# Gate/up of a SwiGLU block as a 2x2 block product with seven products, and the FFN in three parts

## Chip, cores and metric

The kernel runs on one core of a Trainium2 chip. The metric is the device time of one execution in microseconds (us), from the first to the last work of the program; the kernel before has a median of 799.0 us over 3 runs (798.96, 799.0 and 799.23).

## The reference

One transformer-like layer over 512 latent tokens of width 1024 with 256 context tokens. A mixer (attention and a gated recurrence) comes first and isn't touched by the change. The rest is an FFN with 2816 inner features, that is 22 feature tiles of 128, and a last norm:

```python
x = x + gt1 * mix_lat
h2 = modulate(rmsnorm(x, g_norm_ffn[layer]), sh2, sc2)
x = x + gt2 * swiglu(h2, w_gate[layer], w_up[layer], w_down[layer])
return rmsnorm(x, g_final)

def swiglu(h, w_gate, w_up, w_down):
    return (jax.nn.silu(h @ w_gate) * (h @ w_up)) @ w_down
```

All of it is in float32.

## The kernel before, in words

Features lie on the 128 partitions and tokens on the free axis. So that the products keep float32 accuracy, each operand is split into a high part of type fp32r and a low part, which is the rest, and `mm3` (L148) issues three matmuls per 128x128 weight tile: high by high (L150), high by low (L151), low by high (L152).

Weights come in units of 128x1024. `make_unit` (L119) fetches a unit by a DMA on SP's queue into `wf` (three buffers), ACT casts it to the high part `wh` (L132), DVE subtracts it for the low part `wl` (L133). `unit` and `prefetch` make units two or three ahead of their use. A unit holds the eight k-tiles of one feature tile of gate or up, or eight (the last six) of the 22 k-tiles of one output tile of down.

The normalised input h2 is written as `h2h` and `h2l` by `norm2` (L949), first for tokens 0 to 255, then for 256 to 511. `gu_mm` (L989) makes the 24 matmuls of gate or up for one tile, into the two halves of a PSUM tile `big` (two buffers). `gu_act` (L994) then takes silu on ACT, multiplies with up on DVE (L997), and splits into `ah` and `al` (L998 on ACT, L999 on DVE), which hold all 22 tiles. Tiles 0 and 1 run in two halves of 256 tokens, the second beside `norm2(256)`; tiles 2 to 21 have 512 columns. Behind each of these `mods(1)` issues a piece of a modulation vector that is needed later (`late_mod`, L422: a DMA and a DVE product of 128x1024, L427), eight in all.

`ffn_down` (L1020) makes an output tile of 66 matmuls of 512 columns in a PSUM tile `sm` (four buffers), adds it to `x1` (L1028, DVE) and squares it for the last norm (L934 on ACT, L936 on DVE). There are eight; the last runs in two halves of 256 tokens. `final` (L1035) is the last norm of one half: sums over partitions on PE (L174), the inverse root on ACT and DVE (L190 to L182), spread by PE (L216), eight products on DVE (L1041), and the output's DMAs (L1045). `final(0)` is put into the list `side`, which `tick` takes steps from, and so runs beside the last 66 matmuls; `final(256)` comes after them.

The order on each engine is set by the framework's scheduler from the order in which the code issues things and from its own priorities: each engine then runs its list in order and waits at each instruction for what it needs.

Of the kernel before, what the change touches and what calls it, by code (L numbers as in the profile page):

```python
# [10 lines left out]
F32 = mybir.dt.float32  # L11
F32R = mybir.dt.float32r
# [6 lines left out]
P = 128  # L19
# [33 lines left out]
def block_kernel(ctx: ExitStack, tc: tile.TileContext, xT, ctxT, vec, cin, cst, msk, wm, wmt, wi, wqkv, wo, wgu, wd, out):  # L53
# [56 lines left out]
    for u in range(2 * FT):  # L110
        units.append(("wgu", wgu[u], UNIT))
    for n in range(KT):
        for part in range(3):
            w = UNIT if part < 2 else DFF - 2 * UNIT
            units.append(("wd", wd[n][:, part * UNIT : part * UNIT + w], w))
    made = []
    stage = {"pool": L0, "f": 3, "s": 3}

    def make_unit(i):  # L119
        kind, src, w = units[i]  # L120
        f = L0.tile([P, UNIT], F32, tag="wf", name=nm("wf"), bufs=3)
        nc.sync.dma_start(f[:, :w], src)
        if kind == "wo" and i >= WO0 + 4:
            hi = stage["pool"].tile([P, UNIT], F32R, tag="rh", name=nm("rh"), bufs=4)
            lo = stage["pool"].tile([P, UNIT], F32R, tag="rl", name=nm("rl"), bufs=4)
        elif i == GU0 + 3:
            hi = N2.tile([P, UNIT], F32R, tag="xh", name=nm("xh"), bufs=1)
            lo = N2.tile([P, UNIT], F32R, tag="xl", name=nm("xl"), bufs=1)
# [3 lines left out]
        nc.scalar.copy(hi[:, :w], f[:, :w])  # L132
        nc.vector.tensor_sub(lo[:, :w], f[:, :w], hi[:, :w].bitcast(F32))  # L133
        made.append((hi, lo))

    WO0 = NW_IN + 4
    GU0 = WO0 + 8
    WD0 = GU0 + 2 * FT

    def prefetch(n):  # L140
        while len(made) < min(n, len(units)):
            make_unit(len(made))

    def unit(i, ahead=2):
        prefetch(i + 1 + ahead)
        return made[i]

    def mm3(o, L, R, start, stop):  # L148
        (lh, ll), (rh, rl) = L, R
        nc.tensor.matmul(o, lh, rh, start=start, stop=False, skip_group_check=True)  # L150
        nc.tensor.matmul(o, lh, rl, start=False, stop=False, skip_group_check=True)  # L151
        nc.tensor.matmul(o, ll, rh, start=False, stop=stop, skip_group_check=True)  # L152

    def sl(t, f):
        return f(t[0]), f(t[1])
# [771 lines left out]
    def add_sq(key, src, n):  # L927
        if n == 0:
            t = N2.tile([P, 256], F32, tag=f"sqa{key}", name=nm("sqa"), bufs=1)
            sqa[key] = [t]  # L930
            nc.scalar.activation(t, src, AF.Square)
        else:
            t = N2.tile([P, 256], F32, tag="sqt", name=nm("sqt"), bufs=4)
            nc.scalar.activation(t, src, AF.Square)  # L934
            if n < KT - 1:
                nc.vector.tensor_add(sqa[key][0], sqa[key][0], t)  # L936
            else:
                sqa[key].append(t)
# [26 lines left out]

# [17 lines left out]
    side.append(norm2(256))  # L983

    FF = pool("FF", "left")
    ah = FF.tile([P, FT, NL], F32R, name="ah")
    al = FF.tile([P, FT, NL], F32R, name="al")

    def gu_mm(ps, j, u, a, w):  # L989
        for k in range(KT):  # L990
            L = sl(u, lambda t: t[:, k * P : (k + 1) * P])
            mm3(ps[:, j, a : a + w], L, (h2h[:, k, a : a + w], h2l[:, k, a : a + w]), k == 0, k == KT - 1)

    def gu_act(n, ps):  # L994
        sg = FF.tile([P, NL], F32, tag="sgl", name=nm("sgl"), bufs=2)
        nc.scalar.activation(sg, ps[:, 0, :], AF.Silu)
        nc.vector.tensor_mul(sg, sg, ps[:, 1, :])  # L997
        nc.scalar.copy(ah[:, n, :], sg)  # L998
        nc.vector.tensor_sub(al[:, n, :], sg, ah[:, n, :].bitcast(F32))  # L999

    us = [unit(GU0 + i, 3 - i) for i in range(4)]
    pp = [big(), big()]
# [3 lines left out]
            tick()  # L1006
    drain()
    sqa.clear()
    for n in range(2):
        for j in range(2):  # L1010
            gu_mm(pp[n], j, us[2 * n + j], 256, 256)
        gu_act(n, pp[n])
    for n in range(2, FT):
        ps = big()
        for j in range(2):
            gu_mm(ps, j, unit(GU0 + 2 * n + j), 0, NL)
        gu_act(n, ps)
        mods(1)

    def ffn_down(n, a, w):  # L1020
        us = [unit(WD0 + 3 * n + j, 2 - j) for j in range(3)]
        ps = sm()
        for k in range(FT):
            L = sl(us[k // 8], lambda t: t[:, (k % 8) * P : (k % 8 + 1) * P])
            mm3(ps[:, :w], L, (ah[:, k, a : a + w], al[:, k, a : a + w]), k == 0, k == FT - 1)
            if k in (3, 9):
                tick()
        nc.vector.scalar_tensor_tensor(x1[:, n, a : a + w], ps[:, :w], mod[:, 3, n : n + 1], x1[:, n, a : a + w],  # L1028
                                       op0=ALU.mult, op1=ALU.add)
# [129 lines left out]
```

## Time and profile before

| what | value |
|---|---|
| median of the runs | 799.0 us (798.96 to 799.23) |
| the profiled execution, first to last instruction (span) | 793.8 us |
| mean granted TensorE clock | 0.992 |
| PE busy | 771.1 us (97%) |
| DVE busy | 447.4 us (56%) |
| ACT busy | 311.3 us (39%) |
| POOL busy | 7.8 us (1%) |
| gate/up and down | from about 400 us to 783 us |

Durations of single instructions are in nanoseconds where a row says "mean", all else in microseconds. A matmul's row shows 0.40 or 0.28 us, but matmuls overlap in PE's pipeline: what one costs is the distance between the starts of two. The profiled execution has no other time than its span; the runs' median lies 5.2 us above it.

### The profile page before, as it was taken

The numbers are of one execution on the slowest core, as the hardware profiler recorded it, in microseconds if no ns is written. First come the engines' busy times: TensorE is split into PE (matmuls) and PEld (weight loads), VectorE is DVE, ScalarE is ACT, GpSimd is POOL, SyncE is SP. The second block draws the span as 40 slices with busy tenths as digits, with TensorE's granted clock in tenths as the row PEclk, the third lists the DMA queues.
The fourth block names the chain that finished last, engine by engine and source line by source line (L and its number), as shares of the span: only waits on it lengthen the run. The fifth ranks groups of instructions, "written<-read, shape, count | busy, mean of one in ns | idle before, by whom it ended". The sixth has DMA issues, their size and how long they took to land.

```text
span 793.8 us, 10825 instructions
## 1 busy us (share of the span) xinstructions
PE 771.1 (97%) x4342; PEld 629.0 (79%) x4342; DVE 447.4 (56%) x820; ACT 311.3 (39%) x569; POOL 7.8 (1%) x15
## 2 busy tenths in 40 slices
PE   8899999999999989999999999999999999999995
PEld 6568888788887667777999888888888888888885
DVE  5576569739788998885656344423333333233324
ACT  6244345434553587654444233222322232222211
POOL 0000000000000000000000000000000000000000
PEclk8999999999999999999999999999999999999998
DMA  8924723321110023335402334333222323332303
GB/s 329 390 83 140 237 81 107 133 81 54 40 54 28 28 80 107 107 132 194 178 2 80 132 133 159 132 109 97 89 105 82 105 74 100 92 91 84 102 16 107
DMA packets 26706, 88.77 MB, mean 112 GB/s; under 512 B 2976, under 2 KB 5280, under 8 KB 26528
## 3 DMA queue, kind: packets, MB, share of 16 engines
q1 hardware_dynamic: 25568, 87.03, 31.6%
q10 hardware_dynamic: 1088, 1.05, 0.4%
q8 instruction: 34, 0.56, 0.3%
q14 instruction: 16, 0.13, 0.0%
HBM read 85.97 MB, written 2.10 MB: 111 GB/s over the span
## 4 chain that ended last, share of the span: by engine, by line
PE 87%; DVE 6%; DMA 4%; ACT 2%; issue 1%; SPq 0%; DVEq 0%; ACTq 0%
PE big L150 17%; PE big L151 16%; PE big L152 16%; PE sm L150 9%; PE sm L151 9%; PE sm L152 9%; PE big L853 3%; DMA xc<-in_ctxT_dram 1%; PE sm L872 1%; PE sm L604 1%; PE big L854 1%; DMA wm<-in_wm_dram 1%; DMA wms<-in_wm_dram 1%; DVE U L585 1%; PE sm L598 1%
## 5 line engine op out<-in xcount | busy, mean ns | idle before, releaser
L133 DVE TENSOR_TENSOR wl<-wf,wh 128x1024 fp32r<-128x1024 f32 (+2 forms) x100 | 119.7, 1197 | 186.0 <-ACT wh L132 185.9
L132 ACT CAST wh<-wf 128x1024 fp32r<-128x1024 f32 (+2 forms) x100 | 102.9, 1029 | 280.7 <-PE big L151 167.9
L150 PE MATMUL big<-h2h,wh 128*128 128x512 f32 (+1 forms) x368 | 140.3, 381 | 0.0
L151 PE MATMUL big<-h2l,wh 128*128 128x512 f32 (+1 forms) x368 | 140.0, 381 | 0.0
L152 PE MATMUL big<-h2h,wl 128*128 128x512 f32 (+1 forms) x368 | 140.0, 381 | 0.0
L152 PEld LDWEIGHTS big<-h2h,wl 128*128 128x128 f32 x368 | 69.2, 188 | 14.6
L150 PEld LDWEIGHTS big<-h2h,wh 128*128 128x128 f32 x368 | 69.2, 188 | 14.5
L151 PEld LDWEIGHTS big<-h2l,wh 128*128 128x128 f32 x368 | 69.2, 188 | 14.4
L150 PE MATMUL sm<-ah,wh 128*128 128x512 f32 (+1 forms) x198 | 73.5, 371 | 0.0
L152 PE MATMUL sm<-ah,wl 128*128 128x512 f32 (+1 forms) x198 | 73.4, 371 | 0.0
L151 PE MATMUL sm<-al,wh 128*128 128x512 f32 (+1 forms) x198 | 73.4, 370 | 0.0
L427 DVE SCALAR_TENSOR_TENSOR wl<-wl,cs 128x1024 f32<-128x1024 f32 x32 | 39.1, 1222 | 33.2 <-DMA wl<-in_wmt_dram 33.1
L150 PE MATMUL big<-wh,hh 128*128 128x512 f32 x96 | 40.1, 421 | 3.3 <-ACT hh L340 1.9
L150 PEld LDWEIGHTS sm<-ah,wh 128*128 128x128 f32 x198 | 37.3, 188 | 7.1
L151 PEld LDWEIGHTS sm<-al,wh 128*128 128x128 f32 x198 | 37.3, 188 | 7.1
L152 PEld LDWEIGHTS sm<-ah,wl 128*128 128x128 f32 x198 | 37.3, 188 | 7.1
L150 PE MATMUL big<-hh,wh 128*128 128x512 f32 x104 | 42.8, 412 | 0.0
L151 PE MATMUL big<-hl,wh 128*128 128x512 f32 x104 | 40.9, 393 | 0.0
L152 PE MATMUL big<-hh,wl 128*128 128x512 f32 x104 | 40.8, 392 | 0.0
L151 PE MATMUL big<-wl,hh 128*128 128x512 f32 x96 | 38.6, 404 | 0.0
L152 PE MATMUL big<-wh,hl 128*128 128x512 f32 x96 | 38.4, 402 | 0.0
L506 DVE RECIPROCAL G<-S 128x528 f32<-128x528 f32 x8 | 27.5, 3435 | 0.1
(323 smaller groups left out, 1349.5 us busy)
## 6 DMA issues: line engine op xcount, KB each, us to landing
wf<-in_wgu_dram SPq DMA_DIRECT2D x44, 512.0 KB, 3.3
wl<-in_wmt_dram SPq DMA_DIRECT2D x32, 512.0 KB, 3.3
wf<-in_wi_dram SPq DMA_DIRECT2D x25, 512.0 KB, 4.3
wf<-in_wd_dram SPq DMA_DIRECT2D x16, 512.0 KB, 3.5
wms<-in_wm_dram SPq DMA_DIRECT2D x11, 512.0 KB, 9.9
wf<-in_wo_dram SPq DMA_DIRECT2D x8, 512.0 KB, 3.3
wf<-in_wd_dram SPq DMA_DIRECT2D x8, 384.0 KB, 3.0
wm<-in_wm_dram SPq DMA_DIRECT2D x5, 512.0 KB, 10.3
```

Source lines behind the costliest of these rows:

```text
L132: nc.scalar.copy(hi[:, :w], f[:, :w])
L133: nc.vector.tensor_sub(lo[:, :w], f[:, :w], hi[:, :w].bitcast(F32))
L150: nc.tensor.matmul(o, lh, rh, start=start, stop=False, skip_group_check=True)
L151: nc.tensor.matmul(o, lh, rl, start=False, stop=False, skip_group_check=True)
L152: nc.tensor.matmul(o, ll, rh, start=False, stop=stop, skip_group_check=True)
L427: nc.vector.scalar_tensor_tensor(f, f, 1.0, sc, op0=ALU.mult, op1=ALU.mult, accum_out=acc)
L506: nc.vector.reciprocal(I, S)
L585: nc.vector.scalar_tensor_tensor(U[:, c1, :], U[:, c0, :], er[:, 1, c0 : c0 + 1], U[:, c1, :], op0=ALU.mult, op1=ALU.add)
L598: nc.tensor.matmul(t, a2[:, j, :], vt[:, j, h * P : (h + 1) * P], start=True, stop=False, skip_group_check=True)
L604: nc.tensor.matmul(t[g * CH : (g + 1) * CH, :], qg[:, c, :], U[:, c, :], start=False, stop=(g == 1 and d == 1), skip_group_check=True, til ...
L853: nc.tensor.matmul(ps[:, 0, :], L, R[:, :NL], start=(i == 0), stop=(i == 4), skip_group_check=True)
L854: nc.tensor.matmul(ps[:, 1, :NC], L, R[:, NL:], start=(i == 0), stop=(i == 4), skip_group_check=True)
```

## The change

Tiles 0 to 2 stay as they were (`PLAIN = 3`). For tiles 3 to 21 gate and up are seen as one 2x2 block product: the two rows are gate and up, the inner dimension is cut into k-tiles 0 to 3 and 4 to 7, the columns are the tokens 0 to 255 and 256 to 511. Winograd's form of Strassen's product gets the four blocks from seven products of half the size, each of 4 k-tiles by 256 tokens (`gu_pair`: 84 matmuls of 256 columns, where there were 48 of 512). What it needs beside them:

- Sums of weight blocks, once per tile (`make_pair`): s0 and s3 on POOL, s1 and s2 on DVE, in one buffer `ss`; then the casts on ACT and low parts on DVE of four tiles: y (s0, s1), x (the gate unit, tags `wh`, `wl`), z (s2, s3), q (the second half of the up unit).
- Sums of token blocks, once (`h2_sums`): four blocks from h2 on DVE, split into `th` and `tl`. `norm2` writes a float32 copy of h2's second token half for this (`h2f`).
- Sums of products: some are taken in PSUM (a product adds to what is there); the others by copies of a product on ACT (`keep`) and additions on DVE of 256 columns (L1111, L1114, L1117; L1119 and L1122 multiply silu(gate) with up). A product into a half of `big` waits until the product before it in that tile has been read.

The FFN is cut into three parts of 8, 8 and 6 feature tiles: gate/up of a part, then its down product, which adds to `x1`. `ah` and `al` hold one part. The squares are taken in the last part. The steps of `make_pair` are issued by `feed` between the products. The late modulation pieces go two behind each of the tiles 3 to 6. `sqt` has two buffers, before four.

```diff
+    def make_pair(src):
+        fg, fu = [L0.tile([P, UNIT], F32, tag="wf", name=nm("wf"), bufs=3) for _ in range(2)]
+        nc.sync.dma_start(fg, src[0])
+        nc.sync.dma_start(fu, src[1])
+        yield
+        ss = FF.tile([P, 4, 512], F32, tag="ss", name=nm("ss"), bufs=1)
+        nc.gpsimd.tensor_add(ss[:, 0, :], fu[:, :512], fu[:, 512:])
+        nc.gpsimd.tensor_sub(ss[:, 3, :], fg[:, :512], fu[:, :512])
+        yield
+        nc.vector.tensor_sub(ss[:, 1, :], ss[:, 0, :], fg[:, :512])
+        nc.vector.tensor_sub(ss[:, 2, :], fg[:, 512:], ss[:, 1, :])
+        yield
...
+            nc.scalar.copy(hi, src)
+            nc.vector.tensor_sub(lo, src, hi.bitcast(F32))
...
+        y = split(FF, "y", s2[:, :UNIT], 1)
+        yield
+        x = split(L0, "w", fg, 3)
+        yield
+        z = split(FF, "z", s2[:, UNIT:], 1)
+        yield
+        q = split(FF, "q", fu[:, 512:], 1)
...
             nc.scalar.activation(h2h[:, n, a : a + w], t, AF.Identity, bias=s)
+            if a:
+                nc.scalar.activation(h2f[:, n, :], t, AF.Identity, bias=s)
...
+    def h2_sums():
+        yield
+        tr = FF.tile([P, 4, 4, 256], F32, tag="ah", name="tr", bufs=1)
...
+        nc.vector.tensor_sub(tr[:, 2], b22, b12)
+        nc.vector.tensor_sub(tr[:, 0], b12, q(h2h, 0))
+        nc.vector.tensor_sub(tr[:, 0], tr[:, 0], q(h2l, 0))
+        yield
+        nc.vector.tensor_sub(tr[:, 1], b22, tr[:, 0])
+        nc.vector.tensor_sub(tr[:, 3], q(h2h, 1), tr[:, 1])
+        nc.vector.tensor_add(tr[:, 3], tr[:, 3], q(h2l, 1))
+        for i in (0, 1, 2, 3):
...
+            nc.scalar.copy(th[:, i], f)
+            nc.vector.tensor_sub(tl[:, i], f, th[:, i].bitcast(F32))
...
+        prod(pa, a11, lambda k: hq(0, k), True, True)
+        k1 = keep(pa)
+        feed()
+        prod(pb, s1, tq(0), True, True)
+        k5 = keep(pb)
+        feed()
+        prod(pa, s2, tq(1), False, True)
+        k6 = keep(pa)
+        feed()
+        prod(pb, s4, h22, False, True)
+        nc.vector.tensor_add(sg[:, 256:], pb, k6)
+        feed()
+        prod(pa, s3, tq(2), False, True)
+        nc.vector.tensor_add(up, pa, k5)
+        feed()
+        prod(pc, a12, lambda k: hq(1, k), True, True)
+        nc.vector.tensor_add(sg[:, :256], pc, k1)
+        nc.scalar.activation(sg, sg, AF.Silu)
+        nc.vector.tensor_mul(sg[:, 256:], sg[:, 256:], up)
+        feed()
+        prod(pa, a22, tq(3), False, True)
+        nc.vector.tensor_mul(sg[:, :256], sg[:, :256], pa)
+        gu_split(n, sg)
+        feed()
...
+    for n in range(2, KT):
+        gu(n)
+    for n in range(KT):
+        ffn_down(0, n, 0, NL)
+    for n in range(KT, 2 * KT):
+        gu(n)
+    for n in range(KT):
+        ffn_down(1, n, 0, NL)
+    for n in range(2 * KT, FT):
+        gu(n)
...
     for n in range(KT - 1):
-        ffn_down(n, 0, NL)
-    ffn_down(KT - 1, 0, 256)
+        ffn_down(2, n, 0, NL)
+    ffn_down(2, KT - 1, 0, 256)
     side.append(final(0))
-    ffn_down(KT - 1, 256, 256)
+    ffn_down(2, KT - 1, 256, 256)
     side.append(final(256))
```

What stands in a row on DVE in the middle of gate/up, before: the low parts of two units (L133), the product with up (L997), the low part of the activation (L999), tile after tile. Operands are the output, then behind the arrow the inputs.

```order
L133 TENSOR_TENSOR wl_706_5036<-wf_704_5033,wh_705_5035 128x1024
L133 TENSOR_TENSOR wl_711_5072<-wf_709_5069,wh_710_5071 128x1024
L997 TENSOR_TENSOR sgl_707_5063<-sgl_707_5063,big_700_5002 128x512
L999 TENSOR_TENSOR al_3970<-sgl_707_5063,ah_3969 128x512
L133 TENSOR_TENSOR wl_714_5102<-wf_712_5099,wh_713_5101 128x1024
```

And now, in part 2, one turn from the low part of one pair's y to that of the next (lines of the changed kernel: L146 low parts, L137 and L138 the sums s1 and s2, L1073 the activation's low part, the other L11xx evictions of products). The PSUM tile big_789 belongs to the pair ahead, big_807 to the pair whose weights are yl_798, zl_802 and ql_804, and ss_812 to the pair behind.

```order
L146 TENSOR_TENSOR yl_798_5584<-ss_794_5550,yh_797_5583 128x1024
L146 TENSOR_TENSOR wl_818_5728<-wf_805_5655,wh_817_5727 128x1024
L1111 TENSOR_TENSOR sgl_791_5534<-big_789_5532,keep_796_5581 128x256
L1114 TENSOR_TENSOR up_792_5535<-big_789_5532,keep_795_5565 128x256
L1119 TENSOR_TENSOR sgl_791_5534<-sgl_791_5534,up_792_5535 128x256
L146 TENSOR_TENSOR zl_802_5618<-ss_794_5550,zh_801_5617 128x1024
L1122 TENSOR_TENSOR sgl_791_5534<-sgl_791_5534,big_789_5532 128x256
L146 TENSOR_TENSOR ql_804_5637<-wf_788_5529,qh_803_5636 128x512
L137 TENSOR_TENSOR ss_812_5677<-ss_812_5677,wf_805_5655 128x512
L1073 TENSOR_TENSOR al_768_5398<-sgl_791_5534,ah_767_5397 128x512
L138 TENSOR_TENSOR ss_812_5677<-wf_805_5655,ss_812_5677 128x512
L146 TENSOR_TENSOR yl_816_5711<-ss_812_5677,yh_815_5710 128x1024
```

Four rows have become eleven or twelve, and evictions of one pair, which PE waits for, now stand in line with the weight work of the next two. L137 stands behind POOL's addition into the same buffer `ss`, and that behind `zl_802`, the last reader of the buffer's former content.

On PE at a boundary between two tiles, before: the last matmuls into one `big`, then the first into the other.

```order
L150 MATMUL big_732_5266<-h2h_3496,wh_729_5233 128x512
L151 MATMUL big_732_5266<-h2l_3497,wh_729_5233 128x512
L152 MATMUL big_732_5266<-h2h_3496,wl_730_5234 128x512
L150 MATMUL big_740_5332<-h2h_3496,wh_734_5269 128x512
L151 MATMUL big_740_5332<-h2l_3497,wh_734_5269 128x512
L152 MATMUL big_740_5332<-h2h_3496,wl_735_5270 128x512
```

And now between two products of one pair: the last matmul of product s4 (zh, zl with h2), then what stands between, then the first of product s3 (zh with th), which waits for L1111 of this pair on DVE.

```order
L198 MATMUL big_807_5659<-h2h_3496,zl_802_5618 128x256
L196 MATMUL sm_808_5660<-h2h_3496,wh_799_5600 128x256
L197 MATMUL sm_808_5660<-h2l_3497,wh_799_5600 128x256
L198 MATMUL sm_808_5660<-h2h_3496,wl_800_5601 128x256
L196 MATMUL big_825_5786<-h2h_3496,wh_817_5727 128x256
L197 MATMUL big_825_5786<-h2l_3497,wh_817_5727 128x256
L198 MATMUL big_825_5786<-h2h_3496,wl_818_5728 128x256
...
L196 MATMUL big_807_5659<-th_3970,zh_801_5617 128x256
```

Eleven matmuls of 256 columns stand between the two products, three of this pair's own product a12 and eight of the next pair's product a11; before, the other `big` was free for a whole tile.

At the end of the program on DVE, before: the first half's x, the chain of the first `final`, its eight products, and only then the second half's x (L1028).

```order
L1028 SCALAR_TENSOR_TENSOR x1_3492<-sm_859_6245,mod_659,x1_3492 128x256
L191 TENSOR_SCALAR rsv_863_6333<-sm_862_6328 128x2
...
L209 TENSOR_SCALAR rsd_866_6342<-cs_61,rsr_865_6335 128x128
L1041 SCALAR_TENSOR_TENSOR x1_3492<-x1_3492,vc_62,sm_867_6363 128x256 x8
L1028 SCALAR_TENSOR_TENSOR x1_3492<-sm_861_6315,mod_659,x1_3492 128x256
```

And now: both halves' x first (L1169), then the chain (L237 to L255) and the eight products (L1194) of the first half, then those of the second.

```order
L1169 SCALAR_TENSOR_TENSOR x1_3492<-sm_1071_7514,mod_659,x1_3492 128x256
L1169 SCALAR_TENSOR_TENSOR x1_3492<-sm_1073_7536,mod_659,x1_3492 128x256
L237 TENSOR_SCALAR rsv_1075_7548<-sm_1074_7543 128x2
...
L255 TENSOR_SCALAR rsd_1078_7557<-cs_61,rsr_1077_7550 128x128
L1194 SCALAR_TENSOR_TENSOR x1_3492<-x1_3492,vc_62,sm_1079_7569 128x256 x8
L237 TENSOR_SCALAR rsv_1082_7595<-sm_1081_7590 128x2
```

The second half has 18 matmuls, before 66, and its x now stands ahead of the first half's chain.

More of the change, by code (lines that the diff above doesn't have):

```diff
@@ L34 @@
 NW_IN = 25
+PLAIN = 3
 VC = {}
@@ L109, in block_kernel @@
         units.append(("wo", wo[u], UNIT))
[L110 to L114, printed above, removed]
+    GU0 = len(units)
+    pair_at, down_at = {}, {}
+    for part in range(3):
+        for n in range(part * KT, min(FT, (part + 1) * KT)):
+            pair_at[n] = len(units)
+            if n < PLAIN:
+                units += [("wgu", wgu[2 * n], UNIT), ("wgu", wgu[2 * n + 1], UNIT)]
+            else:
+                units.append(("pair", (wgu[2 * n], wgu[2 * n + 1]), UNIT))
+        w = min(UNIT, DFF - part * UNIT)
+        for n in range(KT):
+            down_at[part, n] = len(units)
@@ L119, in make_unit, with feed @@
+    def feed():
+        if not making and len(made) < len(units) and units[len(made)][0] == "pair":
+            making.append(make_pair(units[len(made)][1]))
+        if making and next(making[0], 1):
+            making.clear()
     def make_unit(i):
@@ L126, in make_unit @@
         elif i == GU0 + 3:
[L127 to L128 removed]
+            hi = FF.tile([P, UNIT], F32R, tag="yh", name=nm("yh"), bufs=1)
+            lo = FF.tile([P, UNIT], F32R, tag="yl", name=nm("yl"), bufs=1)
         else:
@@ L136, in block_kernel @@
     WO0 = NW_IN + 4
-    GU0 = WO0 + 8
-    WD0 = GU0 + 2 * FT
     def prefetch(n):
-        while len(made) < min(n, len(units)):
+        while len(made) < min(n, len(units)) and units[len(made)][0] != "pair":
             make_unit(len(made))
@@ L932, in add_sq @@
         else:
-            t = N2.tile([P, 256], F32, tag="sqt", name=nm("sqt"), bufs=4)
+            t = N2.tile([P, 256], F32, tag="sqt", name=nm("sqt"), bufs=2)
             nc.scalar.activation(t, src, AF.Square)
@@ L997, in gu_act, with gu_pair, prod, keep @@
         nc.vector.tensor_mul(sg, sg, ps[:, 1, :])
-        nc.scalar.copy(ah[:, n, :], sg)
-        nc.vector.tensor_sub(al[:, n, :], sg, ah[:, n, :].bitcast(F32))
+        gu_split(n, sg)
+    def gu_pair(n):
+        a11, a12, a22, s1, s2, s3, s4 = made[pair_at[n]]
+        ab, pc = big(), sm()[:, :256]
+        pa, pb = ab[:, 0, :256], ab[:, 1, :256]
+        hq = lambda j, k: (h2h[:, 4 * j + k, 0:256], h2l[:, 4 * j + k, 0:256])
+        h22 = lambda k: (h2h[:, 4 + k, 256:512], h2l[:, 4 + k, 256:512])
+        tq = lambda i: lambda k: sl((th, tl), lambda t: t[:, i, k * 256 : (k + 1) * 256])
+        def prod(o, A, B, start, stop):
+            for k in range(4):
+                mm3(o, sl(A, lambda t: t[:, k * P : (k + 1) * P]), B(k), start and k == 0, stop and k == 3)
+        def keep(src):
+            t = FF.tile([P, 256], F32, tag="keep", name=nm("keep"), bufs=4)
+            nc.scalar.copy(t, src)
+            return t
+        sg = FF.tile([P, NL], F32, tag="sgl", name=nm("sgl"), bufs=2)
+        up = FF.tile([P, 256], F32, tag="up", name=nm("up"), bufs=1)
+        prod(pa, a11, lambda k: hq(0, k), True, True)
[20 more added lines that the diff above has]
+        nc.vector.tensor_mul(sg[:, :256], sg[:, :256], pa)
+        gu_split(n, sg)
+        feed()
     us = [unit(GU0 + i, 3 - i) for i in range(4)]
```

74 lines of the change are left out of this document (58 added, 16 removed).

## Prediction

> **What bounds the kernel now.** I read first the span and clock, then the busy shares and the chain that ended last.
>
> ```profile
> core 0: 793.8 us, clock 0.992
> PE 771.1 (97%) x4342; PEld 629.0 (79%) x4342; DVE 447.4 (56%) x820; ACT 311.3 (39%) x569; POOL 7.8 (1%) x15
> PE 87%; DVE 6%; DMA 4%; ACT 2%; issue 1%; SPq 0%; DVEq 0%; ACTq 0%
> ```
>
> PE is the bound. The runs' median of 799.0 lies 5.2 us above this span; I work in the span and add 5.2 at the end. Next the stretches that the change touches (columns: busy us of PE, PEld, DVE, ACT, POOL, then the clock), and PE's waits from 380 us on.
>
> ```profile
> 400.00:440.00 40.00, 40.00 (x317) 38.82 (x316) 25.55 (x60) 17.54 (x33) 0.00 (x0) 1.00 0.15 54
> 440.00:650.00 210.00, 210.00 (x902) 169.20 (x901) 78.49 (x90) 60.34 (x76) 0.00 (x0) 1.00 0.32 110
> 650.00:770.00 120.00, 120.00 (x531) 97.23 (x530) 36.69 (x45) 28.84 (x40) 0.00 (x0) 1.00 0.28 84
> PE sm L216 <- DVE rsd L209: 1.6, 1, 1.6
> PE sm L174 <- ACT sqt L934: 1.0, 1, 1.0
> ```
>
> From 400 to 770 us PE never stands, at full clock. DVE is busy 78.49 of 210 us in the gate/up stretch (37%), ACT 29%, POOL not at all. So fewer PE cycles are worth their full time, as long as the others stay off PE's path; the change spends just those reserves.
>
> **Change 1: fewer matmul columns (removes).** The cadence of matmuls, from the first and the last row of 45 in a row at 512 columns and of 44 at 256:
>
> ```profile
> 499.61 0.40 PE L150 MATMUL big<-h2h,wh 128*128 128x512 f32 x1
> 509.88 0.40 PE L152 MATMUL big<-h2h,wl 128*128 128x512 f32 x1
> 394.82 0.28 PE L151 MATMUL sm<-onl,rh 128*128 128x256 f32 x1
> 399.87 0.28 PE L152 MATMUL sm<-omh,rl 128*128 128x256 f32 x1
> ```
>
> 10.27/44 = 0.2334 us and 5.05/43 = 0.1174 us: half the columns cost half, though each has its own weight load. A tile was 48 x 0.2334 = 11.20 us; a pair is 7 products x 4 k-tiles x 3 = 84 x 0.1174 = 9.87 us. 1.33 x 19 tiles = **-25.3 us** if PE never waits. The down matmuls are the same in number, only in three parts.
>
> **Change 2: DVE, ACT and POOL work per pair (adds).** Prices:
>
> ```profile
> L133 DVE TENSOR_TENSOR wl<-wf,wh 128x1024 fp32r<-128x1024 f32 x91 | 111.4, 1224 | 181.8 <-ACT wh L132 181.8
> L999 DVE TENSOR_TENSOR al<-sgl,ah 128x512 fp32r<-128x512 f32 x22 | 15.2, 692 | 14.3 <-ACT ah L998 14.3
> L997 DVE TENSOR_TENSOR sgl<-sgl,big 128x512 f32<-128x512 f32 x22 | 15.0, 681 | 0.7 <-ACT sgl L996 0.7
> L936 DVE TENSOR_TENSOR sqa<-sqa,sqt 128x256 f32<-128x256 f32 x24 | 9.3, 421 | 1.8 <-ACT sqt L934 1.6
> L427 DVE SCALAR_TENSOR_TENSOR wl<-wl,cs 128x1024 f32<-128x1024 f32 x32 | 39.1, 1222 | 33.2 <-DMA wl<-in_wmt_dram 33.1
> L132 ACT CAST wh<-wf 128x1024 fp32r<-128x1024 f32 x91 | 95.6, 1050 | 253.5 <-PE big L151 162.6 <-PE sm L151 35.7 <-issue 27.9
> L998 ACT CAST ah<-sgl 128x512 fp32r<-128x512 f32 x22 | 13.7, 621 | 31.6 <-DVE sgl L997 31.6
> L996 ACT ACTIVATE sgl<-big 128x512 f32<-128x512 f32 x22 | 13.0, 590 | 1.4 <-PE big L152 1.4
> L540 ACT COPY cT<-sm 128x256 f32<-128x256 f32 x8 | 3.0, 370 | 4.1 <-PE sm L539 4.1
> L592 POOL TENSOR_TENSOR a<-am,am 128x512 f32<-128x512 f32 x4 | 5.3, 1331 | 196.9 <-DVE am L559 196.9
> wf<-in_wgu_dram SPq DMA_DIRECT2D x44, 512.0 KB, 3.3
> ```
>
> DVE per tile before: 2 x 1.224 + 0.681 + 0.692 = 3.8 us. Per pair after: s1, s2, the low part of q and al, 4 x 0.69; low parts of x, y, z, 3 x 1.22; five 256-wide evictions, 5 x 0.42: **8.5 us of PE's 9.87**. ACT: 3 x 1.05 + 2 x 0.62 + 0.59 + 3 x 0.37 = 6.1 us, hidden. POOL: 2 x 1.28 us. DMA: still 1 MB per tile, 3.3 us to land; the next up unit can be fetched from the second weight sum on, over 4 us ahead of its use: no cost.
>
> Busy time alone would just fit. But DVE runs its list in order, and that list is now a loop of which each turn is one pair: the low part of z frees the one buffer ss; POOL's first add fills it; then come s1 and s2, the low part of the next y, L1111 (which lets product s3 into the PSUM tile), L1114 (which lets product q in), L1119, and the next z. If a turn of this loop takes longer than PE's 9.87 us, it sets the pace, not PE. What a turn takes is worked out with these rows for the spacing of DVE's operations and the way from PE to DVE:
>
> ```profile
> 265.70 0.73 DVE L623 SCALAR_TENSOR_TENSOR onl<-sm,vc,onh 128x512 fp32r<-128x512 f32 x1
> 266.35 1.42 DVE L716 TENSOR_TENSOR kp<-kp,kpm 64x512 f32<-64x512 f32 x1
> 782.79 0.28 PE L152 MATMUL sm<-ah,wl 128*128 128x256 f32 x1
> 783.11 0.48 DVE L1028 SCALAR_TENSOR_TENSOR x<-sm,mod,x 128x256 f32<-128x256 f32 x1 [0.30 <-PE sm L152]
> ```
>
> Back-to-back DVE work starts 0.08 us before the duration is over (265.70 to 266.35 for 0.73), so 12 operations take 7.6 us. Between L1111 and L1114 DVE has nothing else and waits for product s3 (12 x 0.1174 = 1.41 us) and the hand-over from PE (0.32 us), of which I count 1.4. Then about 0.3 us for POOL's 1.28, since L1122 and the low part of q (1.1 us) stand between. Sum 9.3, under 9.87. But the order of two neighbouring pairs differs, PE has only 4 to 13 other matmuls (0.5 to 1.5 us) to put between two products of one tile, and L1111 comes late in the shorter turn: stepping through one such cycle of two pairs by hand, with these durations in the order of each engine's list, I get 1.1 us in which PE waits, **0.5 per pair**. This is my least sure step: an error of 0.1 us in a hand-over comes 19 times.
>
> **Change 3: POOL beside DVE.** The trace has three places where POOL's 512-wide add meets a DVE operation with two operands in SBUF, as nearly all weight sums and low parts are:
>
> ```profile
> 145.56 1.28 POOL L592 TENSOR_TENSOR a<-am,am 128x512 f32<-128x512 f32 x1 [80.55 <-DVE am L559]
> L585 DVE SCALAR_TENSOR_TENSOR U<-U,er x4: 339/347/1307, 145.3 to 147.3; 128x128 f32<-128x128 f32 x4
> 265.95 1.28 POOL L592 TENSOR_TENSOR a<-am,am 128x512 f32<-128x512 f32 x1 [27.58 <-DVE am L559]
> 264.34 0.70 DVE L714 TENSOR_TENSOR kp<-big,cs 64x512 f32<-64x512 f32 x1
> 236.88 1.48 POOL L592 TENSOR_TENSOR a<-am,am 128x512 f32<-128x512 f32 x1 [33.26 <-DVE am L559]
> ```
>
> A DVE operation of 0.35 us took 1307 ns and ended only when POOL's had; kp at 266.35 took 1.42 us where a like one with a PSUM operand took 0.70; in the third place POOL, starting second, was the longer (1.48). So whoever starts second waits. The Trainium skill, page "SBUF — State Buffer", section "Who interferes with whom", states this as a rule: a DVE instruction with two SBUF inputs and a GpSimd instruction that reads SBUF exclude each other for the whole instruction. It speaks against this change, and the trace agrees (1307 beside 347 ns); by it the sum holds the terms that follow, without it the 0.5 us alone.
>
> Here POOL's first add starts as soon as z is done, while DVE does L1122 (one operand in PSUM); then q's low part, two operands in SBUF, waits for the add's end: 0.65 us more in the loop. What the second add does isn't in the trace, where POOL never issues two in a row, so its cost stands between two ends. If the waiting DVE gets in between, the second add takes up to 1.28 us elsewhere: loop 9.95 to 11.2; stepped through, 1.65 us per two pairs, **0.8 per pair**. If POOL's second goes first, DVE loses 1.9 per pair: loop 11.2, with the uneven turns 3.2 per two, **1.6 per pair**. I take the first: at 265.95 to 267.70 DVE got its turn as soon as POOL's one instruction was over, which is nearer to a lock given up after each instruction.
>
> What this makes of the whole: the first pair of parts 2 and 3 is prepared under the down matmuls, so 7 + 5 = 12 pairs pay: 6 us (no lock), **9.6**, or 19.2. In part 1, the ten 1024-wide token sums (12.2 us), 8 late modulation products moved to two per pair (9.8), tile 2's units (2.4), three plain activations (4.1), five pairs (42.7) and three down units (3.7) give DVE 75 us, about 69 back to back, in PE's 2 x 5.6 + 11.2 + 5 x 9.87 = 72: full, with the loop's waits of 1.4 us on top, five times. I put PE's waits there at 5, **8.5** and 11. The extra ACT pass into h2f lies in these. Together 11, **18.1** or 30.2 us; below zero isn't possible, as PE waited for nothing here.
>
> **Change 4: the tail.** Each last half had 66 matmuls, now 18, so the first final no longer hides behind the second half.
>
> ```profile
> 773.67 0.28 PE L152 MATMUL sm<-ah,wl 128*128 128x256 f32 x1
> 776.60 0.16 DVE L191 TENSOR_SCALAR rsv<-sm 128x2 f32<-128x2 f32 x1 [2.12 <-ACT rsr L190]
> 779.58 3.22 DVE L1041 SCALAR_TENSOR_TENSOR x<-x,vc,sm 128x256 f32<-128x256 f32 x8 [1.85 <-PE sm L216]
> 785.32 0.16 DVE L191 TENSOR_SCALAR rsv<-sm 128x2 f32<-128x2 f32 x1 [1.73 <-ACT rsr L190]
> 787.32 3.22 DVE L1041 SCALAR_TENSOR_TENSOR x<-x,vc,sm 128x256 f32<-128x256 f32 x8 [0.87 <-PE sm L216]
> ```
>
> Before: first half's last matmul to the end 793.8 - 773.67 = 20.1. After: the first rstd chain, 2.9 us later before, waits for the second half's x and starts at 3.7; scaling 2.0 later (785.32 to 787.32), 3.2 long, to 8.9; then the second chain and scaling, 2.0, and 6.5 to the end: 17.4. The 48 matmuls now ahead of that point take 5.6: 17.4 + 5.6 - 20.1 = **+2.9** (2 to 4.5). x1 is added up three times, 16 more additions of 512 columns (0.48 us for 256 at 783.11, so under 1), under down matmuls in which DVE is busy 31% (36.69 of 120); each output tile's 18 to 24 matmuls of 512 columns take 4.2 us or more and DVE's work for it is one low part and one addition, under 2.3: nothing, and if that cover went, at most the difference.
>
> **Sum:** -25.3 + 18.1 + 2.9 = -4.3: span 789.5, time **794.7**.
>
> **Rivals.** (1) POOL's pair of adds goes ahead of DVE every time: -25.3 + 30.2 + 2.9 = +7.8, **806.8**, slower. It decides once a pair takes over 11.05 us (9.87 + 1.18 of waits, since 25.3 - 2.9 = 22.4 over 19). For: DVE lost the whole add at 145.56 and 266.35. Against: POOL's second add must win again. (2) No lock that matters, since DVE's evictions have a PSUM operand and fill POOL's time: 11 us of waits, **787.6**. Against: kp at 1.42. (3) PE bound as counted, no waits, -22.4: **776.6**. Against: DVE at 8.5 of 9.87 us in order, with little for PE to put between. That 256-wide matmuls are bound by weight loads is excluded by 0.1174.
>
> **How the numbers follow.** Forecast 0.46, (1) 0.28, (2) 0.18, (3) 0.08. The forecast's own range is 788 to 801 (waits of part 1 and the second add +-4, tail +-1.5). About 0.2% (1.6 us) can be told from no change: 797.4 to 800.6. Of the forecast two thirds lie below, a fifth or less within: faster 0.31 + 0.18 + 0.08 = 0.57, same 0.09, slower 0.34, nearly all from (1). Leaving out most of (3) and the upper third of (1), the range is 783 to 809.
>
> **What would show it.** In the profile after: PE's 256-wide starts 0.1174 apart within a product; pairs 10.7 us apart (10.4 without the lock, 11.4 in (1)); PE waiting for DVE at L1111 and L1114, in turns of two; DVE 512-wide and 1024-wide low parts and sums with means well above 0.69 and 1.22, the maximum 1.28 higher (2.5 in (1)); POOL's adds over 1.28 where DVE got in first; first to last L1194 in one row at the end. I'm wrong if PE waits mainly for ACT or DMA, if low parts keep their durations, or if the tail from the last halves on is no longer than before.

## The result and the profile after

The changed kernel takes 817.6 us (median of 4 runs, 816.5 to 819.3), the kernel before, run together with it, 799.1: a ratio of 1.0234 (95% interval 1.0217 to 1.0250), 18.5 us slower. The forecast was 794.7 in a range of 783 to 809.

The profiled execution of before was about 3.4 us quicker than its other runs: its first gate/up matmul came at 409.8 us, in code that the change doesn't touch, and that of after at 413.9. The granted clock stood at 0.50 from 16 to 22 us in before and from 16 to 29 us in after. A run of after is only 1.8 us longer than its span (819.3 and 817.5), so the 5.2 us between the median and the span of before were mostly that quick execution. The spans are therefore compared from the first gate/up matmul on: 384.0 us before, 403.6 after.

The page of after, its span, busy shares and chain:

```profile
core 0: 817.5 us, clock 0.982
PE 772.3 (94%) x4978; PEld 653.9 (80%) x4978; DVE 579.4 (71%) x998; ACT 368.6 (45%) x676; POOL 63.0 (8%) x53
PE 74%; DVE 14%; ACT 4%; DMA 4%; issue 3%; POOL 0%; SPq 0%; POOLq 0%; DVEq 0%; ACTq 0%
```

The chain was PE for 87% before and is for 74% now; DVE has gone from 6 to 14%. PE waits (from 380 us on), where it waited only in the tail before:

```profile
PE big L196 <- ACT keep L1096: 9.5, 10, 1.8
PE big L196 <- DVE sgl L1111: 9.2, 7, 1.9
PE sm L262 <- DVE rsd L255: 4.5, 2, 2.9
PE big L198 <- DVE yl L146: 0.5, 1, 0.5
```

Product q of the first and of the last pair of part 2, with seven turns between them:

```profile
569.85 0.39 PE L196 MATMUL big<-th,qh 128*128 128x256 f32 x1
653.27 0.30 PE L196 MATMUL big<-th,qh 128*128 128x256 f32 x1
```

83.4 us, or **11.9 per pair**, where a plain tile took 11.2: each pair loses 0.7 us against what it replaced. The forecast had 10.7, its slower rival 11.4. The turns are uneven in twos, as forecast: 12.3, 14.0, 10.9, 13.6, 10.9 and 13.6 us, and 8.3 for the last, which has no next pair's products beside it.

What DVE and POOL do, in groups over the whole FFN:

```profile
L137 DVE TENSOR_TENSOR ss<-ss,wf 128x512 f32<-128x512 f32 x19 | 31.5, 1656 | 8.6 <-POOL ss L134 8.6
L146 DVE TENSOR_TENSOR ql<-wf,qh 128x512 fp32r<-128x512 f32 x19 | 19.9, 1047 | 2.6 <-ACT qh L145 2.3
L138 DVE TENSOR_TENSOR ss<-wf,ss 128x512 f32<-128x512 f32 x19 | 12.9, 680 | 0.1
L135 POOL TENSOR_TENSOR ss<-wf,wf 128x512 f32<-128x512 f32 x19 | 30.0, 1578 | 0.0
L134 POOL TENSOR_TENSOR ss<-wf 128x512 f32<-128x512 f32 x19 | 26.1, 1371 | 423.0 <-DMA wf<-in_wgu_dram 305.6
```

L137, L138 and the low part of q are the same kind of work, 512 columns with two operands in SBUF. L138, which meets no POOL work, has 680 ns; the other two have 1656 and 1047. One turn, in order of time:

```profile
597.96 1.30 POOL L134 TENSOR_TENSOR ss<-wf 128x512 f32<-128x512 f32 x1 [10.94 <-DVE zl L146]
598.41 1.39 DVE L146 TENSOR_TENSOR ql<-wf,qh 128x512 fp32r<-128x512 f32 x1 [0.15 <-ACT qh L145]
599.21 1.74 POOL L135 TENSOR_TENSOR ss<-wf,wf 128x512 f32<-128x512 f32 x1
599.73 1.78 DVE L137 TENSOR_TENSOR ss<-ss,wf 128x512 f32<-128x512 f32 x1
601.43 0.68 DVE L1073 TENSOR_TENSOR al<-sgl,ah 128x512 fp32r<-128x512 f32 x1
602.40 0.28 PE L197 MATMUL big<-h2l,wh 128*128 128x256 f32 x1
603.77 0.41 DVE L1111 TENSOR_TENSOR sgl<-big,keep 128x256 f32<-128x256 f32 x1
604.24 0.38 PE L196 MATMUL big<-th,zh 128*128 128x256 f32 x1 [1.56 <-DVE sgl L1111]
```

POOL's first addition runs 597.96 to 599.26; q's low part starts in it and ends 0.54 us behind it. POOL's second starts at 599.21, before q's part is done, and takes 1.74: it waits in its turn. And s1, started at 599.73, can only work when that second addition is over, at 600.95, and ends at 601.51. The two take turns, and DVE loses in each: 0.7 and 1.1 us. This mutual exclusion of POOL and DVE is called the lock below. At the other end of the line PE's last matmul starts at 602.40, and then PE stands for 1.56 us, until 604.24, for L1111.

### The profile page after: what moved, and what is told of

Its sections match the earlier page's. It is cut to its first block, busy times and chain, and to the rows that moved or that the text cites. A ratio compares the mean times of both kernels' runs of the same rounds, so it can differ in the third digit from the quotient of the medians.

```text
span 817.5 us, 12504 instructions
## 1 busy us (share of the span) xinstructions
PE 772.3 (94%) x4978; PEld 653.9 (80%) x4978; DVE 579.4 (71%) x998; ACT 368.6 (45%) x676; POOL 63.0 (8%) x53
## 3 DMA queue, kind: packets, MB, share of 16 engines
q10 hardware_dynamic: 1088, 1.05, 0.4%
## 4 chain that ended last, share of the span: by engine, by line
PE 74%; DVE 14%; ACT 4%; DMA 4%; issue 3%; POOL 0%; SPq 0%; POOLq 0%; DVEq 0%; ACTq 0%
PE big L196 13%; PE big L197 11%; PE big L198 11%; PE sm L196 9%; PE sm L197 9%; PE sm L198 9%; PE big L899 3%; DMA wf<-in_wgu_dram 2%; DVE ql L146 2%; DVE ss L137 2%; PE sm L918 1%; PE sm L650 1%; PE big L900 1%; PE sm L366 1%; DMA wf<-in_wd_dram 1%
## 5 line engine op out<-in xcount | busy, mean ns | idle before, releaser
L180 ACT CAST wh<-wf 128x1024 fp32r<-128x1024 f32 (+2 forms) x62 | 62.9, 1015 | 134.2 <-PE sm L197 57.0
L181 DVE TENSOR_TENSOR wl<-wf,wh 128x1024 fp32r<-128x1024 f32 (+2 forms) x62 | 73.1, 1178 | 28.5 <-ACT wh L180 27.4
L134 POOL TENSOR_TENSOR ss<-wf 128x512 f32<-128x512 f32 x19 | 26.1, 1371 | 423.0 <-DMA wf<-in_wgu_dram 305.6
L1169 DVE SCALAR_TENSOR_TENSOR x<-sm,mod,x 128x512 f32<-128x512 f32 (+1 forms) x25 | 18.2, 728 | 48.8 <-PE sm L198 48.7
L196 PE MATMUL big<-th,yh 128*128 128x256 f32 x152 | 45.5, 299 | 5.5 <-ACT keep L1096 5.4
L198 PE MATMUL big<-th,yl 128*128 128x256 f32 x152 | 43.0, 283 | 0.5 <-DVE yl L146 0.5
L197 PE MATMUL big<-tl,yh 128*128 128x256 f32 x152 | 42.9, 282 | 0.0
L196 PE MATMUL big<-h2h,wh 128*128 128x256 f32 (+1 forms) x140 | 41.4, 298 | 0.0
L197 PE MATMUL big<-h2l,wh 128*128 128x256 f32 (+1 forms) x140 | 41.3, 296 | 0.0
L198 PE MATMUL big<-h2h,wl 128*128 128x256 f32 (+1 forms) x140 | 41.2, 295 | 0.0
## 6 DMA issues: line engine op xcount, KB each, us to landing
wf<-in_wd_dram SPq DMA_DIRECT2D x8, 384.0 KB, 3.1
```

The lines of the kernel that those rows point to most:

```text
L134: nc.gpsimd.tensor_add(ss[:, 0, :], fu[:, :512], fu[:, 512:])
```

## Experiments

All ratios are to the kernel before, run together with each experiment, with 95% intervals.

**e1: POOL reads nothing.** The two additions become two memsets each, so s0 and s3 are left out.

```diff
-        nc.gpsimd.tensor_add(ss[:, 0, :], fu[:, :512], fu[:, 512:])
-        nc.gpsimd.tensor_sub(ss[:, 3, :], fg[:, :512], fu[:, :512])
+        for j in (0, 3):
+            nc.gpsimd.memset(ss[:, j, :], 0.0)
+            nc.gpsimd.memset(ss[:, j, :], 0.0)
```

> POOL's two additions per pair are replaced by two memsets each, which read nothing; the weight sums s0 and s3 are thereby left out (zeros). Lock theory: in the changed kernel s1 (L137) took 1656 ns and the low part of q 1047 ns, where such operations took 690 before, 1.3 us per pair or 25 us over 19 pairs; with these gone s1 and q fall to about 0.69 and the time falls by 15 to 25 us, to 793 to 803. Rival (PSUM tile): PE's waits come from products that stand behind the reader of the other half of the same PSUM tile; DVE is earlier but ACT's copies are not, so the time falls by 3 to 10 us, to 808 to 815.

Measured: 799.3 us, ratio 1.0009 (0.9984 to 1.0033): 18 us less than the changed kernel. DVE's s1, q and POOL's memsets in it:

```profile
L147 DVE TENSOR_TENSOR ql<-wf,qh 128x512 fp32r<-128x512 f32 x19 | 13.1, 689 | 1.7 <-ACT qh L146 1.5
L138 DVE TENSOR_TENSOR ss<-ss,wf 128x512 f32<-128x512 f32 x19 | 13.1, 688 | 13.8 <-DMA wf<-in_wgu_dram 13.2 <-POOL ss L136 0.6
L135 POOL MEMSET ss<- 128x512 f32 x38 | 18.9, 527 | 422.1 <-DVE zl L147 279.3 <-PE sm L199 142.8
```

Both operations are back at 0.69 beside a POOL that is still busy for 1.05 us at each place. The lock theory's numbers came; the rival's (808 to 815) did not. But the kernel is then no faster than before: a pair of part 2 still takes 10.8 us (75.9 for the same seven turns), not 9.87.

```profile
563.26 0.39 PE L197 MATMUL big<-th,qh 128*128 128x256 f32 x1
639.12 0.37 PE L197 MATMUL big<-th,qh 128*128 128x256 f32 x1
```

**e2: two PSUM tiles.** The halves pa and pb of one tile become tiles of their own.

```diff
-    psum = ctx.enter_context(tc.tile_pool(name="psum", bufs=4, space=bass.MemoryType.PSUM))
+    psum = tc.alloc_tile_pool(name="psum", bufs=4, space=bass.MemoryType.PSUM, reuse_waits="tile")
...
-        ab, pc = big(), sm()[:, :256]
-        pa, pb = ab[:, 0, :256], ab[:, 1, :256]
+        pa, pb, pc = half()[:, :256], half()[:, :256], sm()[:, :256]
...
+    def half():
+        return ps_pool[0].tile([P, 512], F32, tag="half", name=nm("half"), bufs=4)
...
+    ps_pool[0] = tc.alloc_tile_pool(name="psum2", bufs=4, space=bass.MemoryType.PSUM, reuse_waits="tile")
```

The pool of PSUM tiles is opened anew ahead of the pairs, both times with the setting `reuse_waits="tile"`, which it didn't have before. No run has that setting alone, so what it does by itself isn't shown.

> Same work; in the pairs the two halves of the PSUM tile become two tiles of a bank each (four of them, in place of two double ones). PSUM tile theory: product s1 need no longer wait for the copy of a11 (PE waited 9.5 us for copies) nor s3 for L1111 (9.2 us), and the restarts of 0.2 us that go with such waits go too: 15 to 25 us less, 793 to 803. Lock theory: DVE's turn takes 12.2 us per pair as before and PE waits somewhere else for it: under 6 us less, 812 or more.

Measured: 813.4, ratio 1.0199 (1.0152 to 1.0246): 0.35% less, near the lock theory's number, and not clear of noise, since the interval holds the 1.0234 of the changed kernel. PE's waits moved:

```profile
PE half L197 <- ACT keep L1096: 21.7, 14, 3.5
PE sm L263 <- DVE rsd L256: 5.2, 2, 3.6
PE half L197 <- DVE up L1114: 2.4, 2, 2.0
```

L1111 is gone from the list, as it should be; in its place product s2 waits for the copy of a11, which in ACT's list stands behind work that waits for DVE. I read this so: with the lock in place it is DVE's long turn that sets the time, not which wait comes last.

**e3: two buffers for the gate unit.** The gate unit gets a tag of its own.

```diff
-        fg, fu = [L0.tile([P, UNIT], F32, tag="wf", name=nm("wf"), bufs=3) for _ in range(2)]
+        fg = FF.tile([P, UNIT], F32, tag="fg", name=nm("fg"), bufs=2)
+        fu = L0.tile([P, UNIT], F32, tag="wf", name=nm("wf"), bufs=3)
```

> Same work; the gate unit of a pair goes into two buffers of its own, so its fetch no longer waits for the low part of q of the pair before. DMA theory: the cast of the gate unit on ACT, which waited 7 us for the DMA in part 2 and stands ahead of the copies that PE waits for (9.5 us in all), is early, and 6 to 12 us go: 806 to 812. Lock and PSUM tile theories: PE waits for L1111 instead; under 4 us less, 814 or more.

Measured: 816.0, ratio 1.0202 (1.0157 to 1.0246), at most a few us less. The fetch was late, and now isn't. ACT's waits for the gate unit from 555 to 655 us, first in after, then in e3:

```profile
ACT wh L145 <- DMA wf<-in_wgu_dram: 7.0, 5, 2.2
ACT wh L146 <- DMA fg<-in_wgu_dram: 0.7, 2, 0.4
```

But ACT then waits for DVE instead (13.7 us in that stretch of after, 24.4 in e3), and the lock is as it was: q's low part rose to 1314 ns, s1 stayed at 1616. The DMA theory falls.

**e4: three parts, no pairs.** All tiles plain, without token sums and h2f.

```diff
-PLAIN = 3
+PLAIN = 22
...
-    side.append(h2_sums())
```

> No pairs at all: all 22 tiles plain, the FFN in three parts alone, without token sums. What the parts cost by themselves. The prediction's term for the tail was +2.9 us; the two traces show 4.2 us more from the last matmul to the end but fewer matmuls behind the first half: 2 to 5 us more than the kernel before, 801 to 804. If adding to x1 three times or the change from gate/up to down costs PE time: 806 or more.

Measured: 801.3, ratio 1.0031 (1.0009 to 1.0052): 2.5 us (0.7 to 4.2) for the three parts. This is the forecast's term of +2.9. PE has no wait between 380 us and the last norm, so x1's additions and the changes between parts cost PE nothing: from the first gate/up matmul to the last down matmul e4 takes 372.6 us and the kernel before 373.0. What is longer is the end behind it, 14.9 us for 11.0.

**e5: all sums on DVE.** `nc.gpsimd` becomes `nc.vector` in the two lines of e1.

> Same work as the changed kernel; s0 and s3 are added on DVE in place of POOL. Lock theory: DVE lost 1.8 us per pair to POOL's two additions (s1 +0.97 and q's low part +0.36 in duration, the rest as idle time ahead of s1) and now pays 2 x 0.61 to do them itself: some 0.6 us per pair less, 8 to 14 us in all, 803 to 810. Rival (what helped without POOL's reads was that the memsets were short and waited for no fetch, not that DVE was free): DVE only has more to do, 815 to 825.

Measured: 799.0, ratio 1.0011 (0.9985 to 1.0036), 4 us below the lock theory's own range. That range charged the kernel 1.2 us per pair for the two additions that DVE now makes. They cost it nothing: e1, in which no engine makes them, takes 799.3. Without POOL beside it the first of them takes 687 ns:

```profile
L134 DVE TENSOR_TENSOR ss<-wf 128x512 f32<-128x512 f32 x19 | 13.1, 687 | 7.2 <-DMA wf<-in_wgu_dram 7.0
```

DVE does two operations more and the kernel is 18 us faster; the rival of short memsets falls.

**e6 and e7: both edits.** e6 is e1 with e2 (s0 and s3 left out), e7 is e5 with e2 and computes everything.

> The two PSUM tiles of e2 together with the memsets of e1 (weight sums s0 and s3 left out). Without the lock PE still lost 20 us in 74 short waits at the first matmul of a product (0.13 us each and 0.11 behind it). PSUM tile theory: most of these are waits for the reader of the other half, and go: 5 to 10 us of waits are left, 785 to 791. Rival: they are waits for evictions that the product truly needs, or for weights: 12 us or more are left, 793 to 800.

> Same work as the changed kernel; two PSUM tiles, and all four weight sums on DVE. Lock and PSUM tile theories together: no lock, 1.2 us more on DVE per pair (9 us of a pair's 9.87): 790 to 800. If DVE is the bound then, with its waits in order: 803 to 810, no better than e5.

Measured: e6 787.7, ratio 0.9863 (0.9825 to 0.9902); e7 788.6, ratio **0.9878** (0.9841 to 0.9915): faster than both kernels. e6 lies in its expected range, e7 1.4 us below its own. Product q in e7, five pairs apart:

```profile
558.42 0.28 PE L197 MATMUL half<-th,qh 128*128 128x256 f32 x1
608.92 0.28 PE L197 MATMUL half<-th,qh 128*128 128x256 f32 x1
```

10.10 us per pair: 84 matmuls at 0.120 in the mean. Here the pair runs at PE's pace, and its waits are nearly gone:

```profile
PE half L197 <- ACT keep L1096: 3.1, 1, 3.1
PE half L197 <- DVE up L1114: 0.8, 2, 0.5
```

Six kernels make a table of what each obstacle costs, as ratio to before:

| | one PSUM tile | two PSUM tiles |
|---|---|---|
| POOL adds | 1.0234 | 1.0199 |
| POOL reads nothing | 1.0009 | 0.9863 |
| DVE adds | 1.0011 | 0.9878 |

The lock costs 18 us in the one column and 26 in the other; the shared tile some 3 us under the lock, which is not clear of noise, and 11 without it. The lock is the nearer bound and hides most of the other.

**e8: two buffers for ss**, on e7 (`bufs=2`).

> As e7, with two buffers for the weight sums. If the order in which z's low part must come before the next pair's sums holds DVE up: 2 to 6 us less than e7. If not: the same within 1.5 us.

Measured: 789.6, ratio 0.9872 (0.9823 to 0.9921), the same as e7. The one buffer costs nothing once PE sets the pace.

**e10: one POOL addition.** s0 on DVE, s3 on POOL, one PSUM tile.

> Same work as the changed kernel; s0 on DVE, s3 still on POOL (one addition per pair on POOL, not two). My forecast took it that a POOL addition mostly runs where DVE waits anyway; then one addition costs little and this is near e5: 799 to 802. Lock theory, each addition hits the DVE operation that stands beside it: about half of the 18 us are back: 805 to 811.

Measured: 808.5, ratio 1.0134 (1.0096 to 1.0173): about half of the way from e5 to the changed kernel. The one addition now hits s0 (1299 ns here, 687 in e5):

```profile
L134 DVE TENSOR_TENSOR ss<-wf 128x512 f32<-128x512 f32 x19 | 24.7, 1299 | 8.7 <-DMA wf<-in_wgu_dram 8.7
L137 DVE TENSOR_TENSOR ss<-ss,wf 128x512 f32<-128x512 f32 x19 | 14.9, 783 | 0.1
L135 POOL TENSOR_TENSOR ss<-wf,wf 128x512 f32<-128x512 f32 x19 | 27.1, 1427 | 440.4 <-DVE tr L1049 168.6 <-DVE zl L146 140.1 <-DMA wf<-in_wgu_dram 131.6
```

My idea that an addition mostly falls where DVE waits anyway would have given 799 to 802. It falls.

**e11: POOL beside an idle DVE.** The kernel before, with as many POOL additions per tile, into a tile that nothing reads.

```diff
+        if kind == "wgu" and i >= GU0 + 4:
+            scr = FF.tile([P, 512], F32, tag="scr", name=nm("scr"), bufs=1)
+            nc.gpsimd.tensor_add(scr, f[:, :512], f[:, 512:])
```

> The kernel before, with one POOL addition of 512 columns for each unit of gate and up from the third tile on, of two halves of the unit, into a tile that nothing reads: as many POOL additions per tile as in the changed kernel, two, beside a DVE that is busy 37%. Lock theory: the low parts (L133, 1224 ns) get longer by up to 1.3 us each, but DVE has the room and PE waits for none of it: the same time as before within 1.6 us. Rival (POOL's additions cost PE time whatever DVE's load is): 5 us more or above.

Measured: 797.2, ratio 0.9997 (0.9977 to 1.0017). The low parts got longer, and no one minded:

```profile
L133 DVE TENSOR_TENSOR wl<-wf,wh 128x1024 fp32r<-128x1024 f32 x56 | 78.5, 1401 | 151.0 <-ACT wh L132 151.0
L136 POOL TENSOR_TENSOR scr<-wf 128x512 f32<-128x512 f32 x40 | 57.7, 1443 | 306.2 <-DMA wf<-in_wgu_dram 306.2
```

Low parts of units take 1401 ns in the mean, 1224 before. The lock is a loss of DVE's time; it becomes a loss of the kernel's time only where DVE has none to spare.

**e9 and e12: the tail.** On e7, the last three output tiles in halves, 54 matmuls behind the first half; e12 also issues the spread of the first norm three steps later.

```diff
-    for n in range(KT - 1):
+    for n in range(5):
         ffn_down(2, n, 0, NL)
-    ffn_down(2, KT - 1, 0, 256)
+    for n in range(5, KT):
+        ffn_down(2, n, 0, 256)
     side.append(final(0))
-    ffn_down(2, KT - 1, 256, 256)
+    for n in range(5, KT):
+        ffn_down(2, n, 256, 256)
```

> As e7, and the last three output tiles of the last down part run in two halves of 256 tokens, so that 54 matmuls stand behind the first half (18 in e7, 66 before). Tail theory: the first half's last norm hides again; the three-part kernel of e4 was 3.4 us longer than before from the first gate/up matmul to the end, of which 2 to 3 come back: 785 to 787 where e7 is 788.6 on the same scale. If the extra time is the three additions to x1 or the change between parts: the same as e7 within 1 us.

> As e9, with the spread of the first half's norm (L263) issued three steps later, behind 33 of the second halves' 54 matmuls in place of 9. In e9 this spread stood ahead of 45 matmuls and waited 2.1 us for the norm, and the matmuls after it started 0.213 us apart in place of 0.117 for 5 us (granted clock 0.50). Clock theory: without that wait PE stays at full clock, the second half ends 3.5 to 4 us earlier than in e9 and the end comes 3 us earlier: a ratio to the kernel before of 0.982 to 0.985, where e9 had 0.987. If the first half's products on DVE, which now come later, hold the second half's norm instead: the same as e9.

Measured: e9 789.2, ratio 0.9871 (0.9816 to 0.9925); e12 789.4, ratio 0.9900 (0.9867 to 0.9934). Neither can be told from e7, and the first branch of both expectations missed. In e9 the end came 11.2 us after the last matmul, as before the change, so the norm did hide again, but PE paid for it:

```profile
768.45 0.28 PE L199 MATMUL sm<-ah,wl 128*128 128x256 f32 x1
770.86 1.23 PE L263 MATMUL sm<-rsd,ones 128*128 128x128 f32 x4 [2.13 <-DVE rsd L256]
772.31 0.41 PE L199 MATMUL sm<-ah,wl 128*128 128x256 f32 x1
772.52 0.41 PE L197 MATMUL sm<-ah,wh 128*128 128x256 f32 x1
771.00:775.00 4.00, 4.00 (x19) 4.00 (x20) 2.88 (x8) 0.00 (x0) 0.00 (x0) 0.50 0.26 84
```

The spread waited 2.1 us with the second halves queued behind it, and after that wait PE ran at half its clock (0.50) for some 5 us, its matmuls 0.21 us apart. In e12 that wait and the half clock are gone (clock 1.00 from 760 to 775), but then the first half's eight products on DVE stand in front of the second half's last x:

```profile
772.20 3.22 DVE L1201 SCALAR_TENSOR_TENSOR x<-x,vc,sm 128x256 f32<-128x256 f32 x8
775.33 0.48 DVE L1169 SCALAR_TENSOR_TENSOR x<-sm,mod,x 128x256 f32<-128x256 f32 x1
```

So the second branch of e12's expectation came about, and e9's number is that of its second branch, but not for the reason given there. In the profiled executions e12's down part and end are 2.2 us shorter than e9's (49.4 against 51.6 from the last gate/up matmul) and 0.7 shorter than e7's; the runs don't show it.

## Why the prediction was wrong, point by point

**What bounds: right.** Before, PE alone; e4 shows that the three parts by themselves leave it so.

**Change 1, -25.3: nearly right.** In e7 a pair takes 10.10 us, 0.120 us per matmul and not 0.1174, so 19 tiles save at that pace (11.20 - 10.10) x 19 = 20.9 us.

**Change 2, the loop on DVE, 0.5 us of waits per pair: too small.** Without the lock a pair takes 10.8 us in e1, 0.7 above e7's pace and 1.0 above the 9.87 of the sum, where I had 10.4. The step that failed is the cycle stepped through by hand, in which the few matmuls between two products cover most of the evictions. They cover them almost: L1111 and the copies end a moment too late, product after product, because one PSUM tile holds two halves and a product into one waits for the reader of the other. Those many short waits are not in the list above, which shows the long ones, but in the spacing of rows, here ahead of product s1 in after:

```profile
579.42 0.27 PE L196 MATMUL sm<-h2h,wh 128*128 128x256 f32 x1
579.69 0.39 PE L196 MATMUL big<-th,yh 128*128 128x256 f32 x1
579.91 0.28 PE L197 MATMUL big<-tl,yh 128*128 128x256 f32 x1
```

0.27 and then 0.22 us where 0.12 would be: a quarter of a microsecond at a product that hardly waited. With two tiles (e6 against e1) 11 us are back; that this is the tile alone, and not the setting that came with it, isn't shown.

**Change 3, the lock, 0.3 us per pair: the step that failed most.** That POOL and DVE exclude each other was right, and the sentence of the Trainium skill (page "SBUF — State Buffer", section "Who interferes with whom") that it goes by order of issue is what the turn at 597.96 to 601.51 shows. Wrong was the choice between two ends. I took it that a waiting DVE operation gets in between the two additions, and that the second then costs little. It did get in, and the second addition hit the next DVE operation instead, since that was s1, again with two operands in SBUF. In the turn shown the two additions cost DVE 0.7 and 1.1 us of the 1.3 that each takes; over all pairs each costs the kernel about half a microsecond (18 us for 38 of them, and about half of that for 19 in e10). So the loss per pair was rival (1)'s 1.1 us (1.6 less 0.5), though not by its mechanism: 11.9 - 10.8 = 1.1 in part 2, and 18 us in all.

**Part 1, 8.5 us of waits: too small.** The spans from the first gate/up matmul on, cut at the last down matmul of each part, in us:

| | e4, no pairs | after | e1, no lock | e7, neither |
|---|---|---|---|---|
| part 1 (5 pairs) | 136.0 | 144.1 | 136.9 | 138.3 |
| part 2 (8 pairs) | 134.6 | 140.1 | 131.9 | 125.7 |
| part 3 (6 pairs) | 102.0 | 104.3 | 100.0 | 95.4 |
| the rest | 14.9 | 15.2 | 14.9 | 15.4 |

In part 1 the forecast was 6.7 us saved and 8.5 us of waits, so 1.8 more than e4. Measured are 8.1 more; 7.2 of them go with the lock (e1). In parts 2 and 3 the forecast was 18.6 saved and 9.6 of waits, so 9.0 less than e4; measured are 7.8 more. So the waits, counted against the 9.87 us per pair of the sum, come to some 41 us in place of 18.1. With neither obstacle (e7) the pairs of parts 2 and 3 save 15.5 us, their full 1.1 each, but those of part 1 save nothing. DVE is busy there for 56.4 of the 64 us from 440 to 504, which fits the forecast's word that DVE is full; which work holds PE up in part 1 isn't traced further.

**Change 4, +2.9: right.** e4 measured 2.5 (0.7 to 4.2). In after the end comes 18.3 us after the first half's last matmul, forecast 17.4; in the order that was forecast, both halves' x come ahead of the chain.

```profile
799.23 0.28 PE L198 MATMUL sm<-ah,wl 128*128 128x256 f32 x1
799.55 0.48 DVE L1169 SCALAR_TENSOR_TENSOR x<-sm,mod,x 128x256 f32<-128x256 f32 x1
```

**The sum.** With the terms as measured: e7, which has neither obstacle, is 9 us faster than before; the shared PSUM tile takes 10 of that (e5), the lock 18 more. Rival (1) lay nearest with 806.8: right on the lock's size and, like the forecast, short on the waits without it. The range of 783 to 809 ended below the result because both terms, of which I had called the first my least sure step, were bounded by one cycle stepped through by hand, and part 1's by its busy time.

In the spans the difference is 403.6 - 384.0 = 19.6 us: by the table 16.1 are after's against e4 (8.1 in part 1, 7.8 in parts 2 and 3), and 3.5 are e4's against before.

**The signs.** PE's waits at L1111, the uneven turns and the longer means of s1 and q's low part came as written. The sign of being wrong, that PE waits mainly for ACT, half came: 9.5 us for ACT's copies and 9.2 for L1111. e3 shows that the late fetch ahead of those copies isn't the cause.

## What to carry over

Before POOL is given a part of DVE's work, count up to the whole of each addition as time taken from DVE, too, unless DVE idles there (e10, e11). Where PE alternates between two accumulators, give each its own PSUM tile, since in this framework a tile is waited for as a whole (product s3 and L1111 here; e6). And price the short waits at the first instruction of every block, not only the longest wait: here they came to 11 us beside the lock's 18.

## What the runs showed of the hardware that was not expected

- After even a short wait a matmul of 256 columns costs PE more than the wait: its row is 0.39 us long and the next starts 0.22 us behind it, not 0.12 (579.69 above).
- A wait of 2.1 us was enough for PE's clock to fall to half (e9): it is 0.99 from 769 to 770 us and 0.50 from 770 to 771, so it fell 1.3 us into the wait, and matmuls started 0.21 us apart for some 5 us. The Trainium skill, page "TensorE: Matmul & The Clock Gate", section "What's actually happening", speaks of an idle window of about 3.4 us; the row here shows less. In after, a wait of 1.9 us at 497.17 did the same (clock 0.50 from 498 to 500), while a wait of 1.8 us (456.41) and one of 1.6 us (604.24) left the clock at 1.00. So the length of the wait alone doesn't decide; what else decides isn't shown here.

```profile
456.41 0.39 PE L196 MATMUL big<-th,yh 128*128 128x256 f32 x1 [1.80 <-ACT keep L1096]
497.17 0.54 PE L196 MATMUL big<-th,zh 128*128 128x256 f32 x1 [1.91 <-DVE sgl L1111]
497.50 0.41 PE L197 MATMUL big<-tl,zh 128*128 128x256 f32 x1
497.72 0.41 PE L198 MATMUL big<-th,zl 128*128 128x256 f32 x1
```

- POOL and DVE took turns instruction by instruction (597.96 to 601.51 in after); neither kept the other out for two in a row.
